# Seven quarter products instead of eight in 18 gate-and-up blocks of a two-layer diffusion backbone on one core

## The chip, the core and the metric

One NeuronCore of a Trainium2 chip runs the whole program. Its engines are named as in the profile: PE (TensorE, matrix products; PEld is its loading of the stationary operand), DVE (VectorE), ACT (ScalarE), POOL (GpSimd) and SP (SyncE), which issues the transfers. The metric is the time on the device of one execution, in microseconds (us). Lower is better.

## The reference

Two layers. Each has a SwiGLU FFN at half weight, a mixer (attention, spatial gating, retention), and a second FFN. Two streams of 256 tokens each go through: the latent and the context. The last FFN is for the latent alone.

```
D_MODEL = 1024; SEQ = 256; CTX_LEN = 256; DEPTH = 2; D_FF = 2816

def ada_rms(h, w, shift, scale):
    return rms_norm(h, w) * (1.0 + scale) + shift

def swiglu(h, w1, w2):
    g, u = jnp.split(h @ w1, 2, axis=-1)
    return (jax.nn.silu(g) * u) @ w2

def ffn_branch(h, mod, i, nw, w1, w2):
    return h + 0.5 * mod[:, i + 2] * swiglu(ada_rms(h, nw, mod[:, i], mod[:, i + 1]), w1, w2)
```

Everything is float32. Only the first FFN of the second layer is changed.

## The kernel before

Activations lie transposed, features on the 128 partitions: `hTh` and `hTl` hold 8 tiles of features (k tiles) by 512 columns, of which 0 to 255 are the latent's tokens and 256 to 511 the context's. Each float32 operand is kept as two parts of a faster type, a high part (a cast, on ACT) and a low part (the rest, a subtraction on DVE). A product of one k tile is then three matmuls: high by high, high weight by low activation, low weight by high activation (`product`, L200 to L202).

An FFN has 22 blocks of 128 gate and 128 up columns, in two halves of 11 (`JH`). For each block `j` the kernel takes a chunk of gate weights and one of up weights (128 x 1024 each), makes 8 products of 512 columns with each (48 matmuls in all), and gates: SiLU of the gate on ACT (L473), times up on DVE (L474), then the high part `aTh` on ACT (L475) and the low part `aTl` on DVE (L476). After 11 blocks come 8 output tiles `d` of 33 matmuls each (`down`), added to the residual `xT` (L425).

`Stream` feeds the weights in order of use: SP loads a chunk into one of three buffers `wr`, ACT casts it to `wh` (L83), DVE subtracts to `wl` (L94), both with four buffers. Each engine works off its instructions in the order in which the program gives them. That order is written by hand: instructions of DVE, ACT, SP and POOL are put down between the products, and a list of background steps (`bg`) is worked off at a set number of steps per product of 512 columns (`pace`, in `pump`).

In the first FFN of the second layer the first two blocks follow the norm, stream after stream, in products of 256 columns; the norm's tiles become ready among them. From the third block on (`j` = 2) a block is 16 products of 512 columns. The blocks are counted from 0 below. The buffer `cb` holds two rows of inputs for the modulation vectors, which are all finished before this FFN.

## Time and profile before

| | |
|---|---|
| three timed runs | 1847.46 us median, 1846.25 to 1847.79 |
| the profiled execution, first to last instruction | 1845.3 us |
| PE busy | 1819.7 us, 99% of the span |
| PEld busy | 1516.7 us, 82% |
| DVE busy | 1113.1 us, 60% |
| ACT busy | 648.9 us, 35% |
| POOL busy | 127.3 us, 7% |
| DMA engines | 142 GB/s on average |

The profile gives one execution on the chip by its span; the timed runs, made without it, lie 1 to 2.5 us above that span. Busy shares are averages over stages with different limits. Matmuls overlap, so that their own durations add up to more than the time that they take; the time from the start of one to the start of the next is what counts. Idle time stands with the engine that ended it.

### The profile page before, as it was taken

How to read it: one execution, taken by the hardware profiler on the slowest of the kernel's cores; microseconds unless marked ns; L12 is line 12 of the kernel's file. 1: busy time of each engine (PE TensorE's matmuls, PEld its weight loads, DVE VectorE, ACT ScalarE, POOL GpSimd, SP SyncE). 2: the span in 40 equal slices, each digit the busy share in tenths (PEclk: the TensorE clock that was granted, in tenths of full speed). 3: DMA queues.
4: the chain of work that ended last, by engine and by line, in shares of the span. 5: the costliest groups of instructions: out<-in, count | busy, mean ns of one | idle time of the engine just before them, and what ended most of it. 6: DMA issues, size and time to landing. Idle time of an engine off the chain costs nothing. (4 is left out here: it accounts for less than half of the span.)

```text
span 1845.3 us, 25975 instructions
## 1 busy us (share of the span) xinstructions
PE 1819.7 (99%) x10296; PEld 1516.7 (82%) x10296; DVE 1113.1 (60%) x1914; ACT 648.9 (35%) x1051; POOL 127.3 (7%) x153
## 2 busy tenths in 40 slices
PE   7999999999999999999999999999999999999999
PEld 5788888887668988888888898888888867889999
DVE  5787777756445557877777563333334745566665
ACT  3332222235543234222222242222222555354443
POOL 0000000002123400000000000000000103310000
PEclk9999999999999999999999999999999999999999
DMA  7755655333211124645667422222322332335645
GB/s 294 264 185 181 219 183 192 113 116 115 71 56 47 46 92 160 205 165 189 209 227 253 132 99 105 76 97 104 102 75 93 117 102 85 99 126 180 190 172 156
DMA packets 83865, 262.72 MB, mean 142 GB/s; under 512 B 9888, under 2 KB 16672, under 8 KB 83616
## 3 DMA queue, kind: packets, MB, share of 16 engines
q1 hardware_dynamic: 83744, 261.07, 42.0%
q8 instruction: 81, 1.33, 0.3%
q14 instruction: 40, 0.33, 0.1%
HBM read 259.98 MB, written 1.05 MB: 141 GB/s over the span
## 5 line engine op out<-in xcount | busy, mean ns | idle before, releaser
L94 DVE TENSOR_TENSOR wl<-wr,wh 128x1024 fp32r<-128x1024 f32 (+1 forms) x376 | 406.3, 1111 | 106.8 <-ACT wh L83 105.5
L83 ACT CAST wh<-wr 128x1024 fp32r<-128x1024 f32 (+1 forms) x376 | 347.9, 954 | 200.4 <-PE d L201 136.1
L200 PE MATMUL d<-aTh,wh 128*128 128x512 f32 (+1 forms) x770 | 268.9, 349 | 0.0
L201 PE MATMUL d<-aTl,wh 128*128 128x512 f32 (+1 forms) x770 | 268.4, 349 | 0.0
L202 PE MATMUL d<-aTh,wl 128*128 128x512 f32 (+1 forms) x770 | 268.4, 349 | 0.0
L200 PE MATMUL g<-hTh,wh 128*128 128x512 f32 (+2 forms) x736 | 265.4, 361 | 1.6 <-ACT hTh L367 0.6
L201 PE MATMUL g<-hTl,wh 128*128 128x512 f32 (+2 forms) x736 | 265.1, 360 | 1.4 <-DVE hTl L350 1.1
L202 PE MATMUL g<-hTh,wl 128*128 128x512 f32 (+2 forms) x736 | 264.3, 359 | 0.6 <-DVE wl L94 0.5
L202 PE MATMUL u<-hTh,wl 128*128 128x512 f32 (+2 forms) x736 | 264.2, 359 | 0.4 <-DVE wl L94 0.4
L200 PE MATMUL u<-hTh,wh 128*128 128x512 f32 (+2 forms) x736 | 263.6, 358 | 0.0
L201 PE MATMUL u<-hTl,wh 128*128 128x512 f32 (+2 forms) x736 | 263.6, 358 | 0.0
L475 ACT CAST aTh<-sg 128x512 fp32r<-128x512 f32 x66 | 40.9, 619 | 354.2 <-DVE sg L474 354.2
L474 DVE TENSOR_TENSOR sg<-sg,u 128x512 f32<-128x512 f32 x66 | 45.3, 687 | 197.0 <-PE u L202 194.1
L200 PEld LDWEIGHTS d<-aTh,wh 128*128 128x128 f32 x770 | 144.5, 188 | 21.3
L201 PEld LDWEIGHTS d<-aTl,wh 128*128 128x128 f32 x770 | 144.5, 188 | 21.3
L202 PEld LDWEIGHTS d<-aTh,wl 128*128 128x128 f32 x770 | 144.5, 188 | 21.3
L200 PEld LDWEIGHTS g<-hTh,wh 128*128 128x128 f32 x736 | 138.6, 188 | 25.7 <-ACT hTh L367 1.9
L201 PEld LDWEIGHTS g<-hTl,wh 128*128 128x128 f32 x736 | 139.1, 189 | 24.7 <-DVE hTl L350 2.6
L202 PEld LDWEIGHTS g<-hTh,wl 128*128 128x128 f32 x736 | 138.9, 189 | 23.1 <-DVE wl L94 1.7
L201 PEld LDWEIGHTS u<-hTl,wh 128*128 128x128 f32 x736 | 139.1, 189 | 22.2
L202 PEld LDWEIGHTS u<-hTh,wl 128*128 128x128 f32 x736 | 138.9, 189 | 22.2 <-DVE wl L94 0.6
L200 PEld LDWEIGHTS u<-hTh,wh 128*128 128x128 f32 x736 | 138.7, 188 | 21.7
(221 smaller groups left out, 2515.5 us busy)
## 6 DMA issues: line engine op xcount, KB each, us to landing
wr<-in_w_dram SPq DMA_DIRECT2D x176, 512.0 KB, 3.9
aw<-in_ada_dram SPq DMA_DIRECT2D x144, 512.0 KB, 5.2
wr<-in_wi_dram SPq DMA_DIRECT2D x56, 512.0 KB, 3.5
wr<-in_w_dram SPq DMA_DIRECT2D x64, 384.0 KB, 3.6
wr<-in_w_dram SPq DMA_DIRECT2D x64, 320.0 KB, 2.8
wr<-in_wo_dram SPq DMA_DIRECT2D x16, 512.0 KB, 3.6
biasT<-in_bias_dram SPq DMA_DIRECT2D x24, 128.0 KB, 3.5
xT<-in_x_dram SPq DMA_DIRECT2D x2, 512.0 KB, 3.9
```

The source lines that it names most:

```text
L83: self.nc.scalar.copy(out=h[:, :n], in_=self.raw[i][:, :n])
L94: self.nc.vector.tensor_tensor(out=lo[:, :n], in0=t[:, :n], in1=h[:, :n].bitcast(F32), op=ALU.subtract)
L200: PE.matmul(out=ps, lhsT=wh[:, col:col + 128], rhs=hh[rhs_sl], start=start, stop=False)
L201: PE.matmul(out=ps, lhsT=wh[:, col:col + 128], rhs=hl[rhs_sl], start=False, stop=False)
L202: PE.matmul(out=ps, lhsT=wl[:, col:col + 128], rhs=hh[rhs_sl], start=False, stop=stop)
L474: V.tensor_tensor(out=sg, in0=sg, in1=us, op=ALU.mult)
L475: S.copy(out=aTh[:, j], in_=sg)
```

## The change

In blocks 4 to 21 of this FFN, gate and up columns for both streams are taken as one product of 2 x 2 quarters: the two streams (256 columns each), the two halves of the features (four k tiles each), and gate and up. Strassen's scheme (in a form with few additions) makes it in seven quarter products (`Seven.go`), each of 4 k tiles by 256 columns by three matmuls: 84 matmuls of 256 columns in a block in place of 48 of 512.

The scheme needs sums of quarters on both sides. The sums of the activations are made once, in 24 steps on DVE and 8 casts on ACT (`sums`), which are put down as background steps among the products of blocks 2 and 3. The sums of the weights are made for each block: SP loads the up chunk's first half `u0` twice into a part of `cb` (`q`), and two DMAs issued by POOL add the second half `u1` and the gate's first half `g0` to it; after the gate's parts are made, a third adding DMA (`second`) adds half of `q` onto the gate's buffer (then called `r`), and DVE adds that half to the other (`fourth`). The second half of up is loaded once more (`ur`). Per block the parts of `g`, `q`, `r` (1024 columns each) and `u` (512) are made, and six sums and products of the results on DVE and two SiLUs on ACT give the gated block. The work for a block is put down one block ahead, in the places between the seven products (`nxt`, slots 0 to 6).

`Stream` no longer has these blocks' chunks, and runs only up to a limit (`cap`) until the last of them. The gating buffer `sg` has one copy in place of two. Blocks 0 to 3 (`DIRECT`) stay as they were. Line numbers in the diff's file are four to some two hundred higher than before.

```diff
...
+DIRECT = 4
...
+SUMS = 1.0
...
+        self.cap = len(chunks)
...
-                for j in range(JH):
+                for j in range(JH) if (l, f) != (1, 0) else range(DIRECT * (1 - half)):
...
+        class Seven:
+            def __init__(self, pool, l, f):
+                self.pool, self.l, self.f = pool, l, f
+                self.th = pool.tile([128, 4, 4, T], F32R, name="th")
+                self.tl = pool.tile([128, 4, 4, T], F32R, name="tl")
+                self.raw, self.part = {}, {}
+            def sums(self, q):
+                x = []
+                def work():
+                    for tag in ("a", "cu", "ur"):
+                        x.append(self.pool.tile([128, NT], F32, tag=tag, name="sum", bufs=1).rearrange(
+                            "p (k t) -> p k t", k=2))
+                a, b = slice(0, T), slice(T, NT)
+                k0, k1 = slice(2 * q, 2 * q + 2), slice(4 + 2 * q, 6 + 2 * q)
+                def whole(n, k, c):
+                    V.tensor_tensor(out=x[n], in0=hTh[:, k, c].bitcast(F32), in1=hTl[:, k, c].bitcast(F32), op=ALU.add)
+                def parts(i, n, sign=1.0):
+                    h, lo = self.th[:, i, k0], self.tl[:, i, k0]
+                    S.activation(out=h, in_=x[n], func=AF.Copy, scale=sign)
+                    V.scalar_tensor_tensor(out=lo, in0=x[n], scalar=sign, in1=h.bitcast(F32), op0=ALU.mult,
+                                           op1=ALU.subtract)
+                def comb(n, p, r, op):
+                    V.tensor_tensor(out=x[n], in0=x[p], in1=x[r], op=op)
+                return [lambda: (work(), whole(0, k0, b)), lambda: whole(1, k0, a),
+                        lambda: comb(1, 1, 0, ALU.subtract), lambda: parts(0, 1),
+                        lambda: whole(2, k1, b), lambda: comb(0, 2, 0, ALU.subtract), lambda: parts(2, 0),
+                        lambda: comb(2, 2, 1, ALU.add), lambda: parts(1, 2, -1.0),
+                        lambda: whole(0, k1, a), lambda: comb(0, 2, 0, ALU.subtract), lambda: parts(3, 0)]
+            def load(self, j):
...
+                g, u = t_w1[self.l, self.f, j, 0], t_w1[self.l, self.f, j, 1]
+                r = wpool.tile([128, CHUNK], F32, tag="wr", name="wr", bufs=RAW_BUFS)
+                SP.dma_start(out=r, in_=g)
+                q = cb[:, j % 2]
+                for k in range(2):
+                    SP.dma_start(out=q[:, 512 * k:512 * k + 512], in_=u[:, 0:512])
+                G.dma_start(out=q[:, 0:512], in_=u[:, 512:1024], accum_op=ALU.add)
+                G.dma_start(out=q[:, 512:1024], in_=g[:, 0:512], accum_op=ALU.add)
+                self.raw["g", j] = self.raw["r", j] = r
+                self.raw["q", j] = q
+            def load_u(self, j):
...
+                r = self.raw["u", j] = self.pool.tile([128, 512], F32, tag="ur", name="ur", bufs=1)
+                SP.dma_start(out=r, in_=t_w1[self.l, self.f, j, 1][:, 512:1024])
+            def high(self, w, j):
+                if w == "u":
+                    h = self.pool.tile([128, 512], F32R, tag="uh", name="uh", bufs=1)
+                else:
+                    h = wpool.tile([128, CHUNK], F32R, tag="wh", name="wh", bufs=HL_BUFS)
+                S.copy(out=h, in_=self.raw[w, j])
+                self.part[w, j] = [h]
+            def low(self, w, j):
+                h = self.part[w, j][0]
+                if w == "u":
+                    lo = self.pool.tile([128, 512], F32R, tag="ul", name="ul", bufs=1)
+                else:
+                    lo = wpool.tile([128, CHUNK], F32R, tag="wl", name="wl", bufs=HL_BUFS)
+                V.tensor_tensor(out=lo, in0=self.raw[w, j], in1=h.bitcast(F32), op=ALU.subtract)
+                self.part[w, j].append(lo)
+            def second(self, j):
+                G.dma_start(out=self.raw["r", j][:, 0:512], in_=self.raw["q", j][:, 0:512], accum_op=ALU.add)
+            def fourth(self, j):
+                r = self.raw["r", j]
+                V.tensor_tensor(out=r[:, 512:1024], in0=r[:, 512:1024], in1=r[:, 0:512], op=ALU.add)
+            def prepare(self, j):
+                return [lambda: self.high("g", j), lambda: (self.low("g", j), self.second(j)),
+                        lambda: self.high("q", j), lambda: self.low("q", j), lambda: self.fourth(j),
+                        lambda: self.high("r", j), lambda: self.low("r", j)]
+            def product(self, ps, w, j, k, t):
+                wh, wl = self.part[w, j]
+                for n in range(4):
+                    if t in ("x0", "x1", "c0", "c1"):
+                        c = slice(0, T) if t[0] == "x" else slice(T, NT)
+                        th, tl = hTh[:, 4 * int(t[1]) + n, c], hTl[:, 4 * int(t[1]) + n, c]
+                    else:
+                        th, tl = self.th[:, int(t[1]) - 1, n], self.tl[:, int(t[1]) - 1, n]
+                    cw = slice(512 * k + 128 * n, 512 * k + 128 * n + 128)
+                    PE.matmul(out=ps, lhsT=wh[:, cw], rhs=th, start=n == 0, stop=False)
+                    PE.matmul(out=ps, lhsT=wh[:, cw], rhs=tl, start=False, stop=False)
+                    PE.matmul(out=ps, lhsT=wl[:, cw], rhs=th, start=False, stop=n == 3)
+                    pump(T / 512.0)
+            def go(self, j, done, nxt):
+                a = self.pool.tile([128, NT], F32, tag="a", name="a", bufs=1)[:, 0:T]
+                y = self.pool.tile([128, NT], F32, tag="sg", name="sg", bufs=1)
+                w = self.pool.tile([128, NT], F32, tag="cu", name="cu", bufs=1)
+                x, c = slice(0, T), slice(T, NT)
+                b1, ba, bb, bc = mm_bank("p1"), a_bank("p26"), b_bank("p75"), mm_bank("p43")
+                def both(t):
+                    return t.rearrange("p (n t) -> p n t", n=2)
+                def twice(t):
+                    return t.unsqueeze(1).to_broadcast([128, 2, T])
+                self.product(b1[:, x], "g", j, 0, "x0")
+                S.copy(out=a, in_=b1[:, x])
+                nxt(0)
+                self.product(bb[:, c], "q", j, 0, "t1")
+                nxt(1)
+                self.product(ba[:, x], "g", j, 1, "x1")
+                nxt(2)
+                self.product(bb[:, x], "q", j, 1, "t3")
+                nxt(3)
+                self.product(ba[:, c], "r", j, 0, "t2")
+                V.tensor_tensor(out=both(y), in0=both(ba), in1=twice(a), op=ALU.add)
+                S.activation(out=y[:, x], in_=y[:, x], func=AF.Silu)
+                V.tensor_tensor(out=both(w), in0=both(bb), in1=twice(y[:, c]), op=ALU.add)
+                V.tensor_tensor(out=y[:, c], in0=bb[:, x], in1=w[:, c], op=ALU.add)
+                nxt(4)
+                self.product(bc[:, c], "r", j, 1, "c1")
+                nxt(5)
+                self.product(bc[:, x], "u", j, 0, "t4")
+                V.tensor_tensor(out=w, in0=bc, in1=w, op=ALU.add)
+                S.activation(out=w[:, c], in_=w[:, c], func=AF.Silu)
+                V.scalar_tensor_tensor(out=y, in0=w, scalar=-1.0, in1=y, op0=ALU.mult, op1=ALU.mult)
+                done(y, lambda: nxt(6))
...
                 adap[0] = fp
+                seven = Seven(fp, l, f) if (l, f) == (1, 0) else None
+                if seven:
+                    caps = [ws.n_take + 2 * DIRECT, ws.n_take + 2 * DIRECT + 2 * KT, len(ws.chunks)]
+                    ws.cap = caps[0]
                 for half in range(2):
...
                             return gate_raw(j, gs, us)
-                        sg = fp.tile([128, NT], F32, tag="sg", name="sg", bufs=2)
+                        sg = fp.tile([128, NT], F32, tag="sg", name="sg", bufs=1 if seven else 2)
                         S.activation(out=sg, in_=gs, func=AF.Silu)
                         V.tensor_tensor(out=sg, in0=sg, in1=us, op=ALU.mult)
+                        gated(j, sg)
+                    def gated(j, sg, between=None):
                         S.copy(out=aTh[:, j], in_=sg)
+                        if between:
+                            between()
                         V.tensor_tensor(out=aTl[:, j], in0=sg, in1=aTh[:, j].bitcast(F32), op=ALU.subtract)
...
                             ws.prefetch(j + 2)
-                    for j in range(j0, JH):
+                    j1 = DIRECT * (1 - half) if seven else JH
+                    if seven and half == 0:
+                        first_j = seven.prepare(j1)
+                        seven.load(j1)
+                        seven.load(j1 + 1)
+                        bg.extend([s for q in range(2) for s in seven.sums(q)] + [lambda: seven.load_u(j1)])
+                        pace[0], pace[1] = SUMS, 0.0
+                    for j in range(j0, j1):
+                        if seven and j == j1 - 1:
+                            bg.extend(first_j)
                         wg, wu = ws.take(), ws.take(AHEAD - 1)
...
                         gate(j, gs, us)
+                    if seven:
+                        drain_bg()
+                    for j in range(j1, JH if seven else j1):
+                        n = half * JH + j
+                        def nxt(slot):
+                            last_j = j == JH - 1
+                            if slot == 1:
+                                seven.high("u", n)
+                            if slot == 2:
+                                seven.low("u", n)
+                                seven.load_u(n + 1)
+                            if last_j:
+                                if slot == 0:
+                                    ws.cap = caps[half + 1]
+                                    ws.load_to(ws.n_take + RAW_BUFS - 1)
+                                elif slot in (1, 3, 5):
+                                    ws.prefetch((slot + 1) // 2)
+                            elif slot == 0:
+                                seven.high("g", n + 1)
+                            elif slot == 1:
+                                seven.low("g", n + 1)
+                                seven.second(n + 1)
+                            elif slot == 2:
+                                seven.high("q", n + 1)
+                            elif slot == 3:
+                                seven.low("q", n + 1)
+                                if j < JH - 2:
+                                    seven.load(n + 2)
+                            elif slot == 5:
+                                seven.fourth(n + 1)
+                                seven.high("r", n + 1)
+                            elif slot == 6:
+                                seven.low("r", n + 1)
+                        seven.go(n, lambda sg, between: gated(j, sg, between), nxt)
                     def down(m, wa, wb, a, b, ps):
...
                         ps = mm_bank("d")
+                        if seven and half == 0:
+                            if m == KT - 3:
+                                seven.load(JH)
+                                seven.load(JH + 1)
+                            if m >= KT - 2:
+                                for s in seven.prepare(JH)[0 if m == KT - 2 else 4:4 if m == KT - 2 else 8]:
+                                    s()
                         down(m, wa, wb, a, b, ps)
...
```

The first place is DVE from the weights' low parts after block 1's gating on. Names: `wl` is a low part of weights, `sg` and `aTl` the gating of a block, `sum` and `tl` the sums of the activations and their low parts. In brackets stand the engines or DMA lanes whose signal the instruction waits for. Before:

```order
L474 TENSOR_TENSOR sg<-sg,u 128x512 [waits PE_49,Activation_49]
L476 TENSOR_TENSOR aTl<-sg,aTh 128x512 [waits Activation_49]
L94 TENSOR_TENSOR wl<-wr,wh 128x1024 [waits DMAHW6_49,Activation_49]
L94 TENSOR_TENSOR wl<-wr,wh 128x1024 [waits DMAHW7_49,Activation_49]
L474 TENSOR_TENSOR sg<-sg,u 128x512 [waits PE_49,Activation_49]
```

Now, from the second of these `wl` to the first sums, and (behind the line of dots) from the last sums to block 4's first operands (`wl<-wr,wh` of `g`, `wl<-cb,wh` of `q`, `fourth`, `wl` of `r`) and block 3's gating:

```order
L98 TENSOR_TENSOR wl<-wr,wh 128x1024 [waits DMAHW7_49,Activation_49]
L476 TENSOR_TENSOR sum<-hTh,hTl 128x512 x2
L485 TENSOR_TENSOR sum<-sum 128x512 [waits DVE_49]
L481 SCALAR_TENSOR_TENSOR tl<-sum,th 128x512 [waits Activation_49]
...
L485 TENSOR_TENSOR sum<-sum 128x512 [waits DVE_49]
L481 SCALAR_TENSOR_TENSOR tl<-sum,th 128x512 [waits Activation_49]
L527 TENSOR_TENSOR wl<-wr,wh 128x1024 [waits DMAHW0_49,Activation_49]
L527 TENSOR_TENSOR wl<-cb,wh 128x1024 [waits DMASW1_49,DMASW0_49,Activation_49]
L537 TENSOR_TENSOR wr<-wr 128x512 [waits DMASW4_49,DVE_49]
L527 TENSOR_TENSOR wl<-wr,wh 128x1024 [waits PE_49,Activation_49]
L633 TENSOR_TENSOR sg<-sg,u 128x512 [waits PE_49,Activation_49]
L640 TENSOR_TENSOR aTl<-sg,aTh 128x512 [waits Activation_49]
```

24 steps of sums and the four steps of block 4's operands now stand ahead of block 3's gating, with block 2's gating after the 16th sum; each `tl` waits for a cast on ACT that itself waits for the sum before.

The second place is DVE in a block of the new kind (block 5): before, a block was the two gating rows and two `wl` shown above. Now, with the low parts for block 6 among block 5's results:

```order
L527 TENSOR_TENSOR wl<-wr,wh 128x1024 [waits DMAHW0_49,Activation_49]
L527 TENSOR_TENSOR ul<-ur,uh 128x512 [waits DMAHW7_49,Activation_49]
L527 TENSOR_TENSOR wl<-cb,wh 128x1024 [waits DMASW6_49,DMASW7_49,PE_49,Activation_49]
L583 TENSOR_TENSOR sg<-p_9384,a 128x512 [waits DVE_49,PE_49]
L585 TENSOR_TENSOR cu<-p_9385,sg 128x512 [waits DVE_49]
L586 TENSOR_TENSOR sg<-p_9385,cu 128x256 [waits DVE_49]
L537 TENSOR_TENSOR wr<-wr 128x512 [waits DMASW0_49]
L591 TENSOR_TENSOR cu<-p_9386,cu 128x512 [waits DVE_49,PE_49]
L593 SCALAR_TENSOR_TENSOR sg<-cu,sg 128x512 [waits Activation_49]
L527 TENSOR_TENSOR wl<-wr,wh 128x1024
L640 TENSOR_TENSOR aTl<-sg,aTh 128x512 [waits Activation_49]
```

Four steps have become eleven, and the seventh (`fourth`) waits for a DMA that POOL issues.

The third place is POOL in the same stretch, where it had nothing to do before. Now, per block, one `second` and the two additions into `q` for the block after (L502, L503):

```order
L532 DMA wr<-cb 128x512 [waits DMAHW0_49,DMAHW7_49,DMASW6_49,DVE_49]
L502 DMA cb<-in_w_dram 128x512 [waits DMAHW5_49,DMASW1_49]
L503 DMA cb<-in_w_dram 128x512 [waits DMAHW6_49]
L532 DMA wr<-cb 128x512 [waits DMASW4_49,DMASW3_49,DMAHW4_49,DMASW1_49,DVE_49]
L502 DMA cb<-in_w_dram 128x512 [waits DMAHW1_49]
```

`second` waits for the low part of `g` on DVE; the two additions wait for SP's loads of `u0`.

## Rows read from the trace of the kernel before

**Rows 1.** The page: span, and busy us (share) of each engine.

```profile
span 1845.3 us, 25975 instructions
PE 1819.7 (99%) x10296; PEld 1516.7 (82%) x10296; DVE 1113.1 (60%) x1914; ACT 648.9 (35%) x1051; POOL 127.3 (7%) x153
```

**Rows 2.** Windows: stretch, its length, busy us of each engine, granted clock, DMA share, GB/s.

```profile
0.00:50.00 50.00, 38.17 (x334) 28.52 (x335) 27.18 (x69) 17.83 (x36) 1.61 (x6) 1.00 0.81 303
...
1130.00:1180.00 50.00, 50.00 (x217) 40.52 (x216) 15.65 (x17) 12.89 (x17) 0.00 (x0) 1.00 0.26 90
...
1625.00:1630.00 5.00, 3.36 (x21) 3.37 (x22) 2.26 (x4) 2.13 (x4) 1.50 (x2) 0.80 0.20 80
...
1700.00:1750.00 50.00, 50.00 (x425) 50.00 (x424) 31.09 (x45) 22.81 (x31) 0.00 (x0) 1.00 0.58 187
```

**Rows 3.** Timeline of PE: where block 2 begins.

```profile
1100.69 0.39 PE L200 MATMUL g<-hTh,wh 128*128 128x512 f32 x1
```

**Rows 4.** Timeline of DVE: weights split after block 1; gating of blocks 2 and 3.

```profile
1103.49 2.36 DVE L94 TENSOR_TENSOR wl<-wr,wh 128x1024 fp32r<-128x1024 f32 x2 [0.26 <-ACT wh L83]
1112.10 0.69 DVE L474 TENSOR_TENSOR sg<-sg,u 128x512 f32<-128x512 f32 x1 [6.25 <-PE u L202]
1113.47 0.69 DVE L476 TENSOR_TENSOR aTl<-sg,aTh 128x512 fp32r<-128x512 f32 x1 [0.69 <-ACT aTh L475]
...
1123.23 0.69 DVE L474 TENSOR_TENSOR sg<-sg,u 128x512 f32<-128x512 f32 x1 [6.45 <-PE u L202]
```

**Rows 5.** Timeline of DVE, last FFN: output tiles of 33 matmuls of 256 columns.

```profile
1731.44 0.48 DVE L425 SCALAR_TENSOR_TENSOR xT<-d,mod,xT 128x256 f32<-128x256 f32 x1 [1.17 <-PE d L202]
...
1739.14 0.48 DVE L425 SCALAR_TENSOR_TENSOR xT<-d,mod,xT 128x256 f32<-128x256 f32 x1 [1.77 <-PE d L202]
```

**Rows 6.** Groups by line and form, 1100 to 1400 us: busy us, mean ns, idle before.

```profile
L94 DVE TENSOR_TENSOR wl<-wr,wh 128x1024 fp32r<-128x1024 f32 x39 | 46.0, 1221 | 4.5 <-ACT wh L83 4.5
L83 ACT CAST wh<-wr 128x1024 fp32r<-128x1024 f32 x38 | 38.2, 1047 | 11.5 <-PE d L201 11.5
...
L476 DVE TENSOR_TENSOR aTl<-sg,aTh 128x512 fp32r<-128x512 f32 x21 | 14.6, 693 | 14.4 <-ACT aTh L475 14.4
L474 DVE TENSOR_TENSOR sg<-sg,u 128x512 f32<-128x512 f32 x21 | 14.4, 687 | 133.1 <-PE u L202 132.1 <-ACT sg L473 1.0
L475 ACT CAST aTh<-sg 128x512 fp32r<-128x512 f32 x21 | 13.0, 620 | 114.8 <-DVE sg L474 114.8
...
L425 DVE SCALAR_TENSOR_TENSOR xT<-d,mod,xT 128x256 f32<-128x256 f32 x18 | 7.9, 479 | 43.5 <-PE d L202 43.5
```

**Rows 7.** The same view over the whole span, for pieces of 256 columns.

```profile
L463 ACT ACTIVATE sg<-tr 128x256 f32<-128x256 f32 x22 | 11.2, 510 | 38.3 <-DVE tr L461 38.3
...
L467 DVE TENSOR_TENSOR aTl<-sg,aTh 128x256 fp32r<-128x256 f32 x22 | 9.4, 425 | 10.7 <-ACT aTh L466 10.7
...
L466 ACT CAST aTh<-sg 128x256 fp32r<-128x256 f32 x22 | 8.9, 407 | 27.3 <-DVE sg L464 27.3
```

**Rows 8.** DMA issues: engine, count, KB each, median us from issue to landing.

```profile
wr<-in_w_dram SPq DMA_DIRECT2D x176, 512.0 KB, 3.9
aw<-in_ada_dram SPq DMA_DIRECT2D x144, 512.0 KB, 5.2
...
wr<-in_w_dram SPq DMA_DIRECT2D x64, 320.0 KB, 2.8
...
cb<-in_cb_dram SPq DMA_DIRECT2D x1, 1024.0 KB, 8.1
```

**Rows 9.** Timeline of PE: after a stall in the second layer's mixer.

```profile
1626.64 0.44 PE L1225 MATMUL yt<-ident,yR 128*128 128x128 f32 x2 [2.52 <-POOL yR L1017]
...
1628.40 0.41 PE L202 MATMUL op<-hTh,wl 128*128 128x256 f32 x1
1628.61 0.41 PE L200 MATMUL op<-hTh,wh 128*128 128x256 f32 x1
...
1631.53 0.28 PE L202 MATMUL op<-hTh,wl 128*128 128x256 f32 x1
```

More of the change, by code (lines that the diff above doesn't have):

```diff
@@ L98, in high_to @@
     def high_to(self, upto):
-        while self.n_high < min(upto, len(self.chunks)):
+        while self.n_high < min(upto, self.cap):
             self._high()
@@ L106, in load_to @@
     def load_to(self, upto):
-        while self.n_load < min(upto, len(self.chunks)):
+        while self.n_load < min(upto, self.cap):
             self._load()
     def prefetch(self, ahead):
-        while self.n_split < min(self.n_take + ahead, len(self.chunks)):
+        while self.n_split < min(self.n_take + ahead, self.cap):
             self._split()
@@ L442, in tile_hybrid_dit @@
         STR = {(0, 512): (0, 1), (0, 256): (0,), (256, 512): (1,), (256, 514): (0,)}
+        class Seven:
[27 more added lines that the diff above has]
+            def load(self, j):
+                if j >= 2 * JH:
+                    return
+                g, u = t_w1[self.l, self.f, j, 0], t_w1[self.l, self.f, j, 1]
[9 more added lines that the diff above has]
+            def load_u(self, j):
+                if j >= 2 * JH:
+                    return
+                r = self.raw["u", j] = self.pool.tile([128, 512], F32, tag="ur", name="ur", bufs=1)
[69 more added lines that the diff above has]
+                done(y, lambda: nxt(6))
+                for w in "gqru":
+                    self.part.pop((w, j))
+                    self.raw.pop((w, j), None)
```

## The prediction

> **What bounds the kernel now.** I read the page first: PE is busy 1819.7 us of a span of 1845.3 us [rows 1], so only fewer or shorter matmuls can shorten this kernel by much. Then the windows: from 1130 to 1180 us, in the FFN that is changed, PE works without a gap, while DVE is busy 15.65 of 50 us, ACT 12.89, POOL nothing, and the DMA engines a quarter of the time [rows 2]. So this stage has room on every engine but PE. What a matmul costs is read from starts. With 512 columns, a block of 48 matmuls lasts 1123.23 - 1112.10 = 11.13 us, from one gating to the next [rows 4]. With 256 columns, two output tiles of 33 matmuls last 1739.14 - 1731.44 = 7.70 us, 0.1167 us a matmul [rows 5]. In that stage PEld is busy all of the time [rows 2], and still 256 columns cost hardly more than half of 512: the loading of weights stays hidden.
>
> **The change part by part.**
>
> *The products.* A new block has 84 matmuls of 256 columns: 84 x 0.1167 = 9.80 us in place of 11.13, 1.33 us less; 18 blocks give 23.9 us. A product of 12 matmuls lasts 1.40 us.
>
> *The sums of the activations.* Now 24 steps on DVE: 16 sums of 512 columns at 0.69 us [rows 6], and 8 low parts. No row has a `scalar_tensor_tensor` of 512 columns; 256 take 0.48, and a `tensor_tensor` grows from 0.425 to 0.693 [rows 6, 7], so I take 0.75. Before each low part DVE waits for a cast on ACT, as it does for `aTh`: 0.69 us [rows 4]. 16 x 0.69 + 8 x 0.75 + 8 x 0.69 = 22.6 us; steps that need nothing of the one before overlap by nearly 0.1 us, so 22.0. DVE comes to them at 1103.49 + 2.36 = 1105.85 [rows 4], after the weights' low parts. Block 2's gating lies among them, 0.69 + 0.69 + 0.69 = 2.1 us. So the sums end at 1129.9. Block 4's first cast (1.05 us) begins on ACT 0.75 us earlier, at the last cast of the sums, and its low part (1.22 us) ends at 1131.4 [rows 6]. PE would be ready for it at 1100.69 + 2 x 11.13 = 1122.95 [rows 3], and its third matmul wants the low part 0.2 us later: PE waits for 8.2 us. Two more waits follow in block 4. `second` can go only at 1131.4; with 3.9 us for it (below), then `fourth` 0.69, the cast of `r` 1.05, its low part 1.22, and signals, `r` is ready at 1138.4, and its product is due at 1136.8: 1.6 us. And `ul` of block 4 comes behind block 3's gating and block 5's `g` on DVE and ACT (0.69, cast 0.62, a copy of 256 columns 0.41, cast 1.05, low part 1.22, then 0.69 [rows 6, 7]), at 1143.1 for a matmul due at 1141.4: 1.7 us. Together the start costs 11.5 us. Bounds: nothing, if the steps ran at 0.61 us without their waits (24 x 0.61 and the gating end at 1122); and 13.1 us, if the clock costs something. After PE stood still for 2.52 us, matmuls of 256 columns lasted 0.41 us and started 0.21 apart (1.2 GHz) at 1628.40, and lasted 0.28 again (2.4 GHz) at 1631.53 [rows 9]; granted was 0.80 of full speed on average from 1625 to 1630 [rows 2]. That is some 3 us at half pace, 1.6 us lost. Here PE stands still for over 7 us; I count nothing, since block 4 then waits for `r` anyway.
>
> *The steady block on DVE.* Low parts 3 x 1.22, `ul`, `fourth` and `aTl` 3 x 0.69, three results 3 x 0.69, one of 256 columns 0.43, the gating product 0.75: 9.0 us of 9.80. It fits, with no room for waits. One chain closes upon itself from block to block: `fourth` (0.69), the cast of `r` (1.05), the SiLU of 256 columns behind it on ACT (0.51), the gating product (0.75), then on ACT `aTh` (0.62), the copy (0.41) and the next cast of `g` (1.05), the low part of `g` (1.22) [rows 6, 7], and then the adding DMA `second`, for which the next `fourth` waits. That is 6.30 us plus L, the time from the end of `g`'s low part to the landing of `second`. PE sets the pace while L is at most 9.80 - 6.30 = 3.5 us. Beyond that each block is late by L - 3.5: behind `fourth` on DVE stand the results, the gating product, the low part of `r` that PE wants for its fifth product, and the next `g`. There is slack: `r` is ready 0.69 + 0.51 + 0.75 + 1.22 = 3.2 us into a block and wanted at 4 x 1.40 = 5.6, so 2.4 us. Blocks 4 to 10 hand on six times and have no slack left from their start; blocks 11 to 21 hand on ten times and have it. The loss is 16 (L - 3.5) - 2.4 us.
>
> *L.* The trace has no adding DMA and none issued by POOL. `second` moves 256 KB, reading both sides. Nearest rows: a plain load of 320 KB lands after 2.8 us, one of 512 KB after 3.9, one of 512 KB with several others in flight after 5.2, one of 1 MB at the start of the kernel after 8.1 [rows 8]. It handles about as many bytes as a load of 512 KB, so I take 3.9 and keep 2.8 and 8.1 as ends. At 3.9 the loss is 6 x 0.4 + (10 x 0.4 - 2.4) = 4.0 us. The Trainium skill has a price for a transfer issued from GpSimd: "DMA: Bandwidth & Descriptors", section "Anatomy of one DMA — SWDGE (gpsimd) path", fits 2.0 us plus bytes / 436e3 per us, an estimate of 2.6 us for 256 KB; by it nothing would be lost to L, and the sum would be -12.4 us. No row here shows such a transfer, and the fit is not of an adding one.
>
> *What I count as nothing.* The additions into `q`: about 6 us into block n SP starts the loads for block n + 2, and ACT wants `q` 4.7 us into block n + 1, 8.5 us later; two rows of 3.9 just fit, and a delay of 2 us still meets PE's slack. The DMA engines: 1280 KB loaded and 768 KB added per block are 2.1 MB in 9.80 us, 214 GB/s; 303 GB/s took 0.81 of them [rows 2], so they hold about 374, and bytes added would have to cost three times those loaded to fill them. POOL has no other work. The single `sg` is read out long before the next block writes it. Half 1's first operands are made during the last two output tiles, 15 us.
>
> *Sum.* -23.9 + 11.5 + 4.0 = -8.4 us on a span of 1845.3 [rows 1], 1836.9; the runs' median lies 2.2 us above the span, so 1839.
>
> **The rivals.**
>
> *The adding DMA sets the pace (slower).* For it: the chain has eight links on three engines already, and `second` starts just when SP sends 1.3 MB for block n + 2 behind `ul`, so that it is more like the 5.2 us of the modulation's loads than the 3.9. Against it: those loads queue behind each other, this one does not. At 5.2 us: 16 x 1.7 - 2.4 = 24.8 us lost, -23.9 + 11.5 + 24.8 = +12.4, 1860. It decides from L = 4.43, where the sum is nothing (faster by over 0.2% below 4.19, slower by as much above 4.66); at 8.1 us it would be 1906. The same page, section "Issuing engines are not separate DMA queues", says that transfers of all engines share the same 16 DMA engines and interleave, which speaks for this rival; no run yet shows POOL's beside SP's.
>
> *No wait at block 4.* If the casts of the sums come early enough that DVE does not wait for them, the 11.5 us go: -23.9 + 4.0, 1827.5. Against it stands the 0.69 us of each `aTl` [rows 4].
>
> *The sum comes to nothing:* L between 4.19 and 4.66, 1844 to 1851.
>
> **How the numbers follow.** A measurement of this kernel tells about 0.2%, 3.7 us, from no change. Forecast (start dear, L from 2.8 to 4.19, 1835 to 1844): 0.46. No wait at block 4: 0.07. Nothing: 0.13. Slower: 0.34, since L's bounds lie mostly above 4.66, though the two nearest rows by size lie below. So faster 0.53, same 0.13, slower 0.34. The range of 8 in 10 goes from 1828 (no wait at block 4) to 1862 (L = 5.3), which leaves out long adding DMAs; the forecast's own range is the 1835 to 1844 above.
>
> **What would show it.** Matmuls of 256 columns 0.117 us apart in the seven products; PE idle for some 7 us at the start of block 4, ended by DVE's `wl`, and DVE busy without a break from 1106 to 1130 except for casts of `th`; `second` landing 3.9 us after issue; DVE's wait at `fourth` on a DMA under a microsecond; blocks about 10 us apart. It is wrong if `fourth` waits for 2 us or more and PE waits in every block for the low part of `r`, if PE starts block 4 on time, or if matmuls lie further apart than 0.117.

## The result, and the profile after

The changed kernel takes 1874.57 us (median of four, 1872.15 to 1881.24) against 1846.97 for the kernel before beside it: a ratio of 1.0157, 95% interval 1.0138 to 1.0177. I had forecast 1839 and a range up to 1862; it is 27.6 us slower than the kernel before. The profile is of the slowest of the four executions. The span and the busy times on the page of the profile after, and its DMA queues (packets, MB, share of the span of 16 engines):

```profile
span 1879.5 us, 27717 instructions
PE 1815.5 (97%) x10944; PEld 1542.7 (82%) x10944; DVE 1213.8 (65%) x2064; ACT 690.9 (37%) x1131; POOL 174.9 (9%) x207
...
q0 software_dynamic: 7776, 14.16, 4.8%
```

PE is busy about as long as before [rows 1], in shorter matmuls, but it stands still for 64 us in place of 26. The windows show where: before, it had no gap from 1130 to 1180 [rows 2]; after, it idles in each stretch with new blocks, and the granted clock falls as well, to 0.73 in the stretch of the start and to 0.96 in the second half.

```profile
1122.00:1132.00 10.00, 2.96 (x12) 2.24 (x11) 7.03 (x10) 3.77 (x5) 0.86 (x1) 0.73 0.08 26
1132.00:1145.00 13.00, 12.16 (x95) 11.80 (x95) 7.88 (x10) 5.27 (x8) 0.86 (x1) 0.95 0.33 61
1145.00:1160.00 15.00, 13.14 (x108) 12.67 (x107) 9.61 (x13) 5.54 (x9) 2.63 (x3) 1.00 0.77 212
...
1282.00:1420.00 138.00, 116.82 (x891) 111.78 (x890) 92.51 (x122) 55.66 (x88) 24.68 (x28) 0.96 0.67 156
```

(Columns: the stretch and its length; busy us of PE, PEld, DVE, ACT, POOL; granted clock; DMA share; GB/s.) The end of the sums on DVE and the start of block 4 on PE, with the idle time ahead of each instruction in brackets:

```profile
1128.13 0.69 DVE L481 SCALAR_TENSOR_TENSOR tl<-sum,th 128x512 fp32r<-128x512 f32 x1 [0.69 <-ACT th L480]
1129.08 0.58 PE L554 MATMUL p<-hTh,wh 128*128 128x256 f32 x1 [6.58 <-ACT wh L518]
1130.34 0.58 PE L556 MATMUL p<-hTh,wl 128*128 128x256 f32 x1 [0.46 <-DVE wl L527]
1141.47 0.39 PE L556 MATMUL p<-th,ul 128*128 128x256 f32 x1 [0.84 <-DVE ul L527]
```

The first wait is the one that I had predicted: DVE waits for a cast ahead of each low part of the sums, and PE then waits 6.58 + 0.46 = 7.0 us where I had 8.2. Of the two smaller waits, the one for `ul` is 0.84 us for 1.7, and the one for `r` does not show. What I had not predicted is in the blocks behind it. One round of all queues but PE's, from block 5 on (the same timeline; lines with the program's names):

```profile
1151.79 0.68 DVE L527 TENSOR_TENSOR ul<-ur,uh 128x512 fp32r<-128x512 f32 x1
1152.42 0.86 POOL L532 DMA_DIRECT2D wr<-cb  x1 [2.71 <-DMA cb<-in_w_dram]
1152.50 0.33 SPq L511 DMA_DIRECT2D ur<-in_w_dram  x1
1152.88 0.42 SPq L498 DMA_DIRECT2D wr<-in_w_dram  x1
1153.40 1.45 SPq L501 DMA_DIRECT2D cb<-in_w_dram  x2
1154.40 1.05 ACT L518 CAST wh<-cb 128x1024 fp32r<-128x1024 f32 x1 [3.27 <-DMA cb<-in_w_dram]
1155.48 1.23 DVE L527 TENSOR_TENSOR wl<-cb,wh 128x1024 fp32r<-128x1024 f32 x1 [3.02 <-ACT wh L518]
...
1158.88 0.69 DVE L537 TENSOR_TENSOR wr<-wr 128x512 f32<-128x512 f32 x1 [0.38 <-DMA wr<-cb]
...
1160.29 0.88 POOL L502 DMA_DIRECT2D cb<-in_w_dram  x1 [7.00 <-DMA cb<-in_w_dram]
1160.84 1.23 POOL L503 DMA_DIRECT2D cb<-in_w_dram  x1
```

DVE stands still for 3.02 us at the low part of `q` (L527, `wl<-cb`), because ACT's cast of `q` waits 3.27 us for an addition into `cb`. `fourth` (L537), where I had looked for the wait, loses 0.38. Of the 16 new blocks behind the first of each half, the cast of `q` waits in 13, for 2.1 to 4.8 us, and `fourth` in 8, for 0.4 to 2.4. The additions are late because POOL waits for the loads of `q` (7.00 us in the last rows, ahead of the additions for the next block but one), and these go out only when SP has got past `ur`, which needs the low part of `u`. So there is a round trip of two blocks. In 14 of them the medians are: from the end of `u`'s low part in block n to POOL's first addition 7.36 us; from there to ACT's cast of `q` for block n + 2, 6.46; from there to the end of `u`'s low part in block n + 2, 10.73. That is 24.55 us, 12.3 a block (the trips as a whole have the median 24.80 and the mean 25.1). Any path that comes back after two blocks lasts two blocks; what speaks for this one is the waits at its links.

PE's own waits point elsewhere: from block 5 on 20 of 31, 22.7 of 30.8 us, are for the parts of `r`, which I had named as a sign of my rival. But in block 10 `fourth` waits for nothing; DVE had lost 2.71 us at `q` before it, and PE waits for the low part of `r` all the same:

```profile
1204.01 1.23 DVE L527 TENSOR_TENSOR wl<-cb,wh 128x1024 fp32r<-128x1024 f32 x1 [2.71 <-ACT wh L518]
1206.94 0.68 DVE L537 TENSOR_TENSOR wr<-wr 128x512 f32<-128x512 f32 x1
1210.98 0.38 PE L556 MATMUL p<-th,wl 128*128 128x256 f32 x1 [1.19 <-DVE wl L527]
```

### The profile page after: what moved, and what is told of

It is laid out like the page before. It is cut to its first block, busy times and chain, and to the rows that moved or that the text cites. A ratio compares the mean times of both kernels' runs of the same rounds, so it can differ in the third digit from the quotient of the medians.

```text
span 1879.5 us, 27717 instructions
## 1 busy us (share of the span) xinstructions
PE 1815.5 (97%) x10944; PEld 1542.7 (82%) x10944; DVE 1213.8 (65%) x2064; ACT 690.9 (37%) x1131; POOL 174.9 (9%) x207
## 5 line engine op out<-in xcount | busy, mean ns | idle before, releaser
L204 PE MATMUL g<-hTh,wh 128*128 128x512 f32 (+2 forms) x592 | 208.6, 352 | 1.5 <-ACT wh L87 0.5
L205 PE MATMUL g<-hTl,wh 128*128 128x512 f32 (+2 forms) x592 | 208.3, 352 | 1.3 <-DVE hTl L354 1.1
L206 PE MATMUL g<-hTh,wl 128*128 128x512 f32 (+2 forms) x592 | 207.5, 351 | 0.6 <-DVE wl L98 0.5
L206 PE MATMUL u<-hTh,wl 128*128 128x512 f32 (+2 forms) x592 | 207.4, 350 | 0.4 <-DVE wl L98 0.4
L204 PE MATMUL u<-hTh,wh 128*128 128x512 f32 (+2 forms) x592 | 207.0, 350 | 0.0
L205 PE MATMUL u<-hTl,wh 128*128 128x512 f32 (+2 forms) x592 | 206.9, 350 | 0.0
L205 PEld LDWEIGHTS d<-aTl,wh 128*128 128x128 f32 x770 | 144.5, 188 | 21.2
L206 PEld LDWEIGHTS d<-aTh,wl 128*128 128x128 f32 x770 | 144.5, 188 | 21.2
L278 DVE CUSTOM_DVE_ANT_0 aw<-aw,cb 128x1024 f32<-128x1024 f32 x128 | 155.0, 1223 | 2.4
L212 PE MATMUL nat<-wh,hTh 128*128 128x512 f32 (+2 forms) x384 | 137.1, 357 | 0.0
L214 PE MATMUL nat<-wh,hTl 128*128 128x512 f32 (+2 forms) x384 | 128.0, 333 | 0.4 <-DVE hTl L354 0.4
L213 PE MATMUL nat<-wl,hTh 128*128 128x512 f32 (+2 forms) x384 | 127.7, 333 | 0.0
```

The costliest lines, as they stand in the source:

```text
L204: PE.matmul(out=ps, lhsT=wh[:, col:col + 128], rhs=hh[rhs_sl], start=start, stop=False)
L205: PE.matmul(out=ps, lhsT=wh[:, col:col + 128], rhs=hl[rhs_sl], start=False, stop=False)
L206: PE.matmul(out=ps, lhsT=wl[:, col:col + 128], rhs=hh[rhs_sl], start=False, stop=stop)
L212: PE.matmul(out=ps, lhsT=hh[lhs_sl], rhs=wh[:, wc], start=start, stop=False)
L213: PE.matmul(out=ps, lhsT=hh[lhs_sl], rhs=wl[:, wc], start=False, stop=False)
L214: PE.matmul(out=ps, lhsT=hl[lhs_sl], rhs=wh[:, wc], start=False, stop=stop)
```

## The experiments

**Theory 1:** this round trip over `q` sets the pace. **Theory 2** (my rival): the adding DMA `second`, in the chain that closes from block to block, does. **Theory 3:** the DMA engines are too slow altogether. "Block" below is the mean of ten periods in the second half, from the first to the last of the 11 rows `COPY a<-p` on ACT. In the kernel after it is 12.94 us. Ratios are to the kernel before as it ran beside each: 1845.32 us for the first four rows, 1847.88 for the next four, 1845.35 for the last four.

| kernel | us, median | ratio, 95% interval | block, us |
|---|---|---|---|
| direct6 | 1867.64 | 1.0119 (1.0104 to 1.0134) | 12.64 |
| early_loads | 1854.41 | 1.0044 (1.0029 to 1.0059) | 11.22 |
| q_plain | 1850.53 | 1.0025 (1.0015 to 1.0035) | 11.14 |
| no_second | 1853.15 | 1.0042 (1.0026 to 1.0058) | 11.37 |
| no_adds | 1834.65 | 0.9929 (0.9912 to 0.9945) | 10.03 |
| pool_second | 1853.11 | 1.0029 (1.0020 to 1.0039) | 11.43 |
| early_pool | 1840.62 | 0.9962 (0.9947 to 0.9976) | 10.57 |
| early_pool6 | 1836.06 | 0.9937 (0.9921 to 0.9953) | 10.57 |
| order_late | 1874.55 | 1.0159 (1.0143 to 1.0174) | 12.75 |
| order_dma | 1833.78 | 0.9946 (0.9932 to 0.9959) | 9.92 |
| order_dma6 | 1833.40 | 0.9939 (0.9927 to 0.9952) | 10.02 |
| order_dve6 | 1830.98 | 0.9926 (0.9912 to 0.9939) | 10.17 |

**direct6: the start.**

```
-DIRECT = 4
+DIRECT = 6
```

> Six blocks are made in the old way before the seven products begin, in place of four. If the sums of the activations come too late (the prediction's start term), the waits of 6.6, 2.5 and 0.8 us in the first new block go, and two blocks of about 12.2 us become 11.1: 10 to 13 us faster than the changed kernel, 1862 to 1865 us. If that time would be lost to the chains of the weight sums anyway, 2 us at most: 1872 us.

6.9 us less than after: under what I expected of the start's wait, over what I expected without it. Blocks stayed slow, so the start is not the cause of the loss.

**early_loads, q_plain, no_second: one chain at a time.** The first splits `load`: SP's part goes to slot 0, POOL's two additions (`adds`) stay in slot 3. The others take lines out: q_plain leaves out a part of `q`'s sum and no_second a part of `r`'s, so they serve for times alone.

```
 early_loads, in nxt:
+    if slot == 0 and j < JH - 2:
+        seven.load(n + 2, False)
...
-        seven.load(n + 2)
+        seven.adds(n + 2)
 q_plain, in load:
-    G.dma_start(out=q[:, 0:512], in_=u[:, 512:1024], accum_op=ALU.add)
-    G.dma_start(out=q[:, 512:1024], in_=g[:, 0:512], accum_op=ALU.add)
 no_second, in second:
-    G.dma_start(out=self.raw["r", j][:, 0:512], in_=self.raw["q", j][:, 0:512], accum_op=ALU.add)
```

> SyncE's loads for block n + 2 are put down at the start of block n, ahead of the load of ur, in place of after the low part of u; GpSimd's two additions into q stay where they were. Theory 1 (the chain over two blocks from those loads over the additions to the cast of q sets the pace): the chain is 4 to 5 us shorter over two blocks, so a block can get 2 us shorter, down to the next bound: 1840 if that is TensorE, 1855 to 1862 if it is the adding DMA of r. Theory 2 (the adding DMA of r sets the pace already, as my rival had it): no change, 1870 to 1876. Theory 3 (the DMA engines are too slow altogether): no change either.

> Leaves out both additions into q, so that q's products lack a part of their weights. Theory 1: the cast of q no longer waits for a DMA and blocks get to 10 to 11 us, 1838 to 1856 us. Theory 2: the adding DMA of r is as before or a little shorter, with little else in its queue; 1862 to 1874.

> Leaves out the adding DMA into r, so that r lacks a part of its weight sum. Theory 1: the chain over q stays, 1866 to 1875 us; VectorE goes on waiting 2 to 3 us in each block at the low part of q. Theory 2: blocks get to 10 us, 1836 to 1842 us. Theory 3: a third of the added bytes gone, something between.

q_plain came out as theory 1 has it, and early_loads 0.6 us under what it gives with the next bound behind it. no_second fits neither theory 1 nor theory 2, only the "something between" of theory 3, which order_dma below rules out: taking away `second` helped nearly as much. That points to two chains of almost the same length, and no single cause. With the early loads `q` is on time, and now `fourth` waits in every block. DVE in early_loads:

```profile
1319.77 1.23 DVE L534 TENSOR_TENSOR wl<-wr,wh 128x1024 fp32r<-128x1024 f32 x1 [0.17 <-ACT wh L525]
...
1326.05 0.69 DVE L544 TENSOR_TENSOR wr<-wr 128x512 f32<-128x512 f32 x1 [1.53 <-DMA wr<-cb]
...
1330.82 1.22 DVE L534 TENSOR_TENSOR wl<-wr,wh 128x1024 fp32r<-128x1024 f32 x1 [0.17 <-ACT wh L525]
...
1337.05 0.69 DVE L544 TENSOR_TENSOR wr<-wr 128x512 f32<-128x512 f32 x1 [1.49 <-DMA wr<-cb]
```

From the end of `g`'s low part, 1321.00, to `fourth`, 1326.05, L is 5.05 us; from there to the end of the next low part, 1332.04, 5.99. Together 11.04: the chain that I had put at 6.30 + L. In no_second DVE no longer waits at `fourth`, and the wait is ACT's for `q` again:

```profile
1319.98 1.05 ACT L518 CAST wh<-cb 128x1024 fp32r<-128x1024 f32 x1 [1.89 <-DMA cb<-in_w_dram]
...
1331.52 1.05 ACT L518 CAST wh<-cb 128x1024 fp32r<-128x1024 f32 x1 [2.28 <-DMA cb<-in_w_dram]
```

Its round trip has the medians 5.84 + 6.21 + 10.60 = 22.65 us, 11.3 a block. Without `second` it is 1.9 us shorter, 1.5 of it in the loads. The landings of SP's transfers agree, first after, then no_second, 1275 to 1400 us (KB each, median us from issue to landing):

```profile
wr<-in_w_dram SPq DMA_DIRECT2D x9, 512.0 KB, 5.7
cb<-in_w_dram SPq DMA_DIRECT2D x18, 256.0 KB, 5.8
cb<-in_w_dram POOLq DMA_DIRECT2D x18, 256.0 KB, 4.7
wr<-cb POOLq DMA_DIRECT2D x10, 256.0 KB, 5.7
```

```profile
wr<-in_w_dram SPq DMA_DIRECT2D x9, 512.0 KB, 4.3
cb<-in_w_dram SPq DMA_DIRECT2D x18, 256.0 KB, 4.4
```

**no_adds, pool_second, early_pool, early_pool6: both chains, and the addition on GpSimd.** no_adds is q_plain and no_second together, for times alone. The others compute the addition into `r`:

```
-    G.dma_start(out=self.raw["r", j][:, 0:512], in_=self.raw["q", j][:, 0:512], accum_op=ALU.add)
+    r = self.raw["r", j]
+    G.tensor_tensor(out=r[:, 0:512], in0=r[:, 0:512], in1=self.raw["q", j][:, 0:512], op=ALU.add)
```

early_pool has the early loads besides, and early_pool6 `DIRECT = 6` as well.

> Leaves out all three adding DMAs (q and r lack parts of their weight sums); everything else stays. Both theories: neither chain waits for a transfer, and a block lasts as long as its 84 matmuls, 9.8 us by the prediction, or the 9.5 us of VectorE: 18 x 1.33 us less than before, and most of the start's 8 to 11 us more, so 1831 to 1836. If blocks stay at 11 us, neither adding DMA was the cause, but the order on VectorE and ScalarE.

> Only the adding DMA of r becomes a GpSimd addition of 128x512 (1.5 us for such a tile in the kernel before). If two chains of about 11 us each were there (q's and r's), this is as leaving that DMA out: 1851 to 1857 us, with ScalarE waiting for the addition into q. If the adding DMA of r alone was at fault: 1836 us. As GpSimd now also waits for the loads of q ahead of the next r, up to 3 us worse.

> Both chains shortened: the loads for block n + 2 at the start of block n, and the addition into r on GpSimd as a computation. If those two chains are all, blocks go to the 9.8 us of TensorE and the time to 1832 to 1838 us (18 x 1.3 less than before, the start's wait more). If VectorE is the next bound with its 8.5 us and 1.05 us of waits, the same; if GpSimd's addition slows VectorE down, 1840 or more.

> As the kernel before it in this list, with six old blocks ahead of the seven products in place of four. The start's wait of 9 us goes, and two blocks more are 1.3 us longer: 6 to 7 us less than with four, 1825 to 1831 us. If the start's wait is hidden by then, 3 us more than with four.

no_adds fits both theories: from its second block on, a block of the second half lasts 9.92 or 9.93 us and PE has no gap (windows):

```profile
1282.00:1420.00 138.00, 138.00 (x978) 128.91 (x977) 97.08 (x136) 59.55 (x98) 0.00 (x0) 1.00 0.37 121
```

The kernel after loses 39.9 us to its adding DMAs. Leaving one chain alone costs 18.5 (q's, no_second) or 15.9 (r's, q_plain). These are differences of medians against no_adds, whose kernel before was the slower one; by the ratios they are 42, 21 and 18. pool_second comes out as no_second, so a `second` that is no transfer leaves `q`'s chain at the same length. early_pool, with both chains cut, is faster than before, but stays at 10.53 us a block, and early_pool6 gains 4.6 us on it where I expected 6 to 7. DVE and POOL in early_pool6:

```profile
1328.65 1.61 POOL L540 TENSOR_TENSOR wr<-wr,cb 128x512 f32<-128x512 f32 x1 [7.17 <-DVE wl L534]
1329.03 2.32 DVE L534 TENSOR_TENSOR wl<-cb,wh 128x1024 fp32r<-128x1024 f32 x1
```

DVE's low part lasts 2.32 us in place of 1.23 beside GpSimd's addition, and ends 1.09 after that ends. The Trainium skill's "GPSIMD Engine Reference", section "1. Specifications", says that GpSimd's access to SBUF is shared with VectorE and contends with instructions that read two inputs from there; these two rows agree. In five blocks of early_pool6 (1300 to 1352.65 us) DVE is busy for 9.3 us of each 10.53, and waits for ACT take most of the rest, so it has no room left.

**order_late, order_dma, order_dma6, order_dve6: another order.** Ahead of the gating product DVE waits 0.88 us for ACT's SiLU, then ACT 0.76 for the product, and the cast of the next `g` stands behind that. This edit fills the two waits with the low part of `r` and the cast of `g` for the block after next:

```
     S.activation(out=w[:, c], in_=w[:, c], func=AF.Silu)
+    nxt(6)
     V.scalar_tensor_tensor(out=y, in0=w, scalar=-1.0, in1=y, op0=ALU.mult, op1=ALU.mult)
-    done(y, lambda: nxt(6))
+    done(y, lambda: nxt(7))
...
     elif slot == 6:
         seven.low("r", n + 1)
+        if j < JH - 2:
+            seven.high("g", n + 2)
+    elif slot == 7 and j < JH - 2:
+        seven.low("g", n + 2)
+        seven.second(n + 2)
```

Slots 0 and 1 do this only for the first new block of a half. order_late has this alone, order_dma the early loads besides, order_dma6 `DIRECT = 6` too, and order_dve6 makes the addition into `r` on DVE ahead of `fourth`.

> The changed kernel with another order alone: g of the block after next is cast right behind the SiLU and split behind the gating product, so that the adding DMA of r starts 1 us earlier against the next addition and its chain no longer closes from block to block. Loads and both additions into q as in the changed kernel. If q's chain stands by itself, blocks stay at 11.2 to 12 us and the time at 1851 to 1866 us; if r's chain was the one that counted, 1836 us.

> That order together with the early loads; all three adding DMAs stay DMAs. Neither chain closes within a block any more, so, if the two chains are the whole cause, blocks fall to the 9.93 us that they last without any adding DMA: 1833 to 1837 us. If instead the transfers themselves slow something down (DMA engines, GpSimd), blocks of 10.5 us and more: 1843 us or more.

> As the kernel before it in this list, with six old blocks in place of four: the start's wait of 7 us goes, and two blocks are 1.2 us longer each. 4 to 5 us less: 1828 to 1832 us.

> The same with the addition into r on VectorE, 0.69 us more there and a transfer less. VectorE then has 9.1 us of work in 9.93: if the blocks are bound by TensorE, the same time as the kernel before it within 2 us; if VectorE's waits can't all be filled, 1 to 3 us more.

order_late came out as I expected for neither chain: it takes as long as the kernel after, 8.6 us more than the most that I gave for `q`'s chain by itself. I had also taken `r`'s chain to be open now. It still closes from block to block, but 1.2 us shorter: from `fourth` to the end of the next low part of `g` 4.81 us where it was 5.99. `r`'s chain is shorter and the time does not move, so `r`'s is not the one that sets the pace. The two are linked, though: `second` reads half of `q`. In every second block of the second half it goes out only 0.54 us after the addition into that half has landed, 2.4 to 3.8 us behind the low part of `g` in place of 0.3, and `fourth` then loses up to 3.2 us. In the second half the blocks behind the first alternate between 9.2 to 10.1 and 14.8 to 15.9 us, and every second cast of `q` waits (ACT):

```profile
1335.49 0.37 ACT L574 COPY a<-p 128x256 f32<-128x256 f32 x1
1336.27 1.05 ACT L518 CAST wh<-cb 128x1024 fp32r<-128x1024 f32 x1
...
1344.70 0.37 ACT L574 COPY a<-p 128x256 f32<-128x256 f32 x1
...
1350.28 1.05 ACT L518 CAST wh<-cb 128x1024 fp32r<-128x1024 f32 x1 [4.70 <-DMA cb<-in_w_dram]
...
1360.11 0.36 ACT L574 COPY a<-p 128x256 f32<-128x256 f32 x1
1360.89 1.05 ACT L518 CAST wh<-cb 128x1024 fp32r<-128x1024 f32 x1
```

1335.49 to 1360.11 is 24.62 us for two blocks, about the round trip of the kernel after. So theory 1 holds for the kernel after, with `r`'s chain right behind it. order_dma has all three adding DMAs, moves more bytes in this stretch than the kernel after (165 GB/s for 156), and its blocks last 9.92 us on average, without a gap on PE, which rules theory 3 out:

```profile
1282.00:1420.00 138.00, 138.00 (x977) 128.92 (x976) 97.75 (x137) 59.95 (x98) 21.74 (x25) 1.00 0.66 165
```

It is 40.8 us faster than the changed kernel, and than order_late beside it, and 0.54% faster than before. order_dma6 was to be 4 to 5 us better still and is 0.4 (1.3 by the ratios). In the traces PE still waits 3.3 us in six places at its start, where order_dma waits 8.1, and its two old blocks take 2.4 us longer, which leaves 2.4 to gain; the rest is open. order_dve6, at 0.9926, is the fastest I ran; its distance to order_dma6 lies inside their intervals.

## Why the prediction was wrong

**The step that failed** is the one that I counted as nothing: the additions into `q`. I gave them a window of 8.5 us and 2 of slack, 10.5 in all, and took two rows of 3.9 us [rows 8], a load and an addition. The rows after show 7.36 us to the landing of the loads (`ur` and `g`'s 512 KB go out ahead of them, 1.25 MB in all) and 6.46 for two additions one behind the other: 13.8 us. The row of 1 MB with 8.1 us, which I kept only as an end for L, was the nearer one for the loads. Nor did I follow this chain round: it comes back to itself after two blocks over `u`'s low part, so that slack does not take up the lateness; it is paid in each of the 16 blocks that follow another.

**The rival that pointed the right way named the wrong DMA.** `second` was not what the kernel after waited for most, but its chain was second in line. The sign that I had named, PE waiting for `r` in every block, does not tell the two apart: in no_second, where no transfer adds to `r`, 13 of PE's 15 waits from block 5 on are still for `r`. My formula for the chain held in its shape: 5.99 + L where I had 6.30 + L; L was mis-sized, 5.05 with the loads out of its way, not 3.9. With these two and a block of 9.93 us on PE it gives 16 x (5.99 + 5.05 - 9.93) - 2.4 = 15.4 us, where I had 4.0; q_plain lies 15.9 us above no_adds (18 by the ratios), and early_loads, from which L is taken, 19.8 (21), so the formula is somewhat low. The Trainium skill's fit ("DMA: Bandwidth & Descriptors", "Anatomy of one DMA — SWDGE (gpsimd) path") gives an estimate of 2.6 us for `second`. No adding DMA here is that short; the medians are 4.0 us and more. What the rival drew on from the same page of the Trainium skill, "Issuing engines are not separate DMA queues", agrees with the landings above: SP's loads take 1.4 us longer when `second` is in flight.

**The products.** A block of 84 matmuls lasts 9.93 us, 0.118 apart, where I had 9.80 from [rows 5]: 18 x 1.20 = 21.6 us saved, not 23.9.

**The start.** PE's waits at block 4 are 7.9 us in all for my 8.2 + 1.6 + 1.7 = 11.5; no wait for `r` shows on PE. The rival without a wait at block 4 is out, since each low part of the sums waits 0.7 us for its cast. (My bound of no wait at all left out that a cast and a low part follow the sums, some 1 us.) The clock, counted as nothing, costs something: in no_adds, where PE waits for 7.0 us, 98 matmuls take 13.0 us from 1132 to 1145 at a clock of 0.86, 1.4 more than at 0.118 apart: 8.4 us in all. no_adds is 12.3 us under the kernel before (13.2 under the one beside it) where the products give 21.6, which leaves 9.3 us (8.4) for the start.

**The sum with the terms as the runs size them:** -21.6 + 9.3 + 39.9 = +27.6, against my -23.9 + 11.5 + 4.0. Only the last term was far off; the errors of the first two, 2.3 and 2.2 us, happen to cancel. The 9.3 and the 39.9 are differences of medians, so that the sum comes out by construction. The traces check them: 8.4 us for the start, as just said, and for the blocks 6 x (12.02 - 9.93) + 10 x (12.94 - 9.93) = 42.6 us, with the mean periods of the two halves. The profiled spans of after and no_adds, each the slowest of its four, differ by 45.0 us: 31.0 of them is PE standing still, and 14.0 PE's busy time, 1815.5 and 1801.5 for the same 10944 matmuls. That part is what waits cost besides themselves: from 1282 to 1420 us a clock of 0.96 for 1.00 is, as an estimate, 0.04 x 138 = 5.5 us, and the rest fits the restarts. PE waits 33 times in the new blocks behind the start; behind each the second matmul starts some 0.22 us after the first, not 0.12, and ahead of each the last matmul counts its whole 0.28 us: 33 x (0.10 + 0.16) = 8.6.

**The two chains together** cost 39.9 and not the 18.5 of the longer one, since `q`'s round trip is longer beside `second`: by the means of the 14 trips 25.1 us, where no_second has 22.8. Of the 2.3 us, 1.45 lie in the loads, 0.2 in the additions and 0.65 on the way back, where `fourth` stands. 16 x 1.16 = 18.6 us, with the 18.5 37.1. In 7 rounds of the kernel after, too, `second` goes out 0.54 us after an addition into `q` has landed, up to 1.5 us late, so that `r`'s chain takes on `q`'s lateness. **Still open:** the other 3 us, and what in the way back is the waits of `fourth`, which no run separates.

## What to carry to other kernels

A transfer is hidden only if its whole round trip (what releases it, what goes out ahead of it in its queue, the landing, and the way back) fits into as many blocks as it spans; add up that trip from rows before counting it as nothing. Where two chains are about as long, removing either seems to gain the same; cut both, and look at which wait is left. Here the same adding DMAs, started earlier and with a low part and a cast moved into two waits, turned +1.6% into -0.5%.

## What the runs showed of the hardware

An adding DMA of 256 KB landed 4.0 us (order_dma) to 6.0 us (order_late) after issue where it was `second`, and 5.7 in the kernel after; those into `q` took 4.7 there and 7.5 in early_loads, where they overlap with `second` (medians of the second half's blocks). POOL's instruction alone lasts 0.87 to 1.6 us.

Behind short waits the granted clock fell. Four windows of the kernel after, and one of order_late (columns as above):

```profile
1300.00:1302.00 2.00, 0.66 (x6) 0.45 (x5) 0.13 (x1) 1.04 (x1) 0.00 (x0) 1.00 1.05 175
1302.00:1304.00 2.00, 1.24 (x9) 1.04 (x10) 1.97 (x3) 0.21 (x1) 0.00 (x0) 1.00 0.96 307
1304.00:1306.00 2.00, 2.00 (x12) 2.00 (x11) 0.84 (x2) 0.20 (x1) 0.21 (x1) 0.50 0.87 219
1306.00:1308.00 2.00, 2.00 (x14) 2.00 (x13) 0.78 (x2) 0.01 (x1) 1.57 (x2) 0.65 0.42 55
...
1282.00:1420.00 138.00, 123.95 (x913) 120.02 (x913) 92.77 (x124) 55.47 (x88) 24.56 (x28) 0.91 0.67 157
```

PE stood still for 2.1 us of the first four, in two waits; then it worked without a gap, but from 1304.1 to 1307.3 at the lower of its two levels (1.2 GHz, matmuls 0.21 apart), and at 2.4 GHz after that. In order_late, with waits of up to 3.8 us, the clock from 1282 to 1420 is 0.91 on average: an estimate of 0.09 x 138 = 12.4 us lost for the 5.5 of the kernel after, though PE stands still there for 14.1 us only (138 - 123.95), and for 21.2 after.
